# Alternating the two heads of a pair in three groups of small matmuls of a hybrid RWKV-7 block

## The chip, the cores and the metric

The kernel runs on one core of one Trainium2 chip. The metric is the device time of one execution in microseconds; the kernel before was timed three times, with a median of 1982.09 us (1978.47 to 1982.77). The profile is of one execution, and its times are counted from the first instruction of the span.

## The reference, cut to what matters

One layer of a diffusion backbone works on 256 context tokens and 256 latent tokens of 2048 features. A modulated norm is followed by one input projection, whose columns feed three groups: a bidirectional RWKV-7 recurrence (16 heads of 64 features), a short convolution and a Fourier mixing. Their outputs go through one output projection and a gated residual; a SwiGLU feed-forward layer with 5632 hidden features and a last norm follow. The change touches only the recurrence, which for each head and direction is

```
sa  = S · (-kk_t)
S   = S * w_t + sa ⊗ (kk_t * a_t) + v_t ⊗ k_t
y_t = S · r_t
```

with a 64 x 64 state S per head. The context's final states start the scans of the latent tokens; only the latent tokens need y.

## The kernel before, in words

The program has three stages: `phase_a` and `phase_kv` (modulation vectors, norms, first projections and keys), `recurrence`, and `phase_ffn`. Nearly all weights are multiplied as a high and a low part, three matmuls for each K-tile (`mm3`, `mm6`); `wblock` loads a block and splits it.

`recurrence` treats the heads in eight pairs, two heads of 64 features side by side on the 128 partitions (`HV[0]` and `HV[1]` are partitions 0 to 63 and 64 to 127). It goes over the eight pairs for the context stream (`s = 0`), then over the eight for the latent stream (`s = 1`): sixteen passes. The 256 tokens of a pass are cut into four chunks of 64 (`NC = 4`, `C = 64`). A pass has four running parts, written as Python generators: `rw_prep` (scaled keys and queries, Gram blocks, token-major values), two `rw_inverse` (the inverse of a triangular 64 x 64 matrix, one for each direction), and `rw_scan` (the state over the chunks), which for the latent stream ends in `rw_out` (the output y).

The loop of `recurrence` goes round by round: each running part makes one step, up to its next `yield`, and the number yielded is the share of TensorE, in microseconds, that the step is charged. `tick` then issues pieces of the filling products (value, query, gate, convolution, Fourier and output projections; tile `pj`) until the round has reached about 2.2 us (`ROUND_C`, `ROUND_L`). On TensorE the order of instructions is exactly the order in which the program issues them (`manual_schedule` for that engine); on the other engines a planner orders them by a simulated timeline. The charges are constants of the code: the token-major values have no charge of their own, the Gram blocks are charged 0.6 us (context) or 1.0 us (latent) a direction, `rw_out` 2.2 us.

Three places matter.

Lines 589 to 597 bring the values of a pair into token-major order, chunk by chunk, into the PSUM tile `pv` (tag `pp`): the even head by a matmul with a 64 x 64 unit matrix, the odd head by TensorE's transpose (line 595). ScalarE copies the tile out afterwards.

Lines 626 to 642 make the Gram blocks, direction by direction. For each head a PSUM tile `pg` (tag `pp`, two buffers for all users of the tag) takes four products, one a chunk, of 64 partitions by 128 stationary columns; then VectorE reads it, once for `ga` and for the latent stream once more for `mq`. So the first head's tile is read while TensorE works at the second head's. What takes a buffer of `pp` next (the other direction, then the transposed keys `pt` at line 645) waits for these reads.

`rw_out` (lines 831 to 850) sums, for each chunk, head and direction, two products into `py` (tag `acc`): `UV` times `MQ` with 128 rows and 64 columns of the array, and the state `w` times `AQ` with 64 rows and 64 columns. It goes through chunk, head, direction, and for each takes first the one, then the other.

Of the kernel before, what the change touches and what calls it, by code (L numbers as in the profile page):

```python
# [10 lines left out]
F32 = mybir.dt.float32  # L11
# [4 lines left out]
PSUM = bass.MemoryType.PSUM  # L16

P = 128
# [4 lines left out]
C = 64  # L23
# [35 lines left out]
class Cols:  # L59
    """Column map of a packed [128, n] array."""  # L60
# [140 lines left out]
class Builder:  # L201
# [12 lines left out]
    def wide(self, dt):  # L214
        """The place with room for two more columns a K-tile."""
        return self.t(self.cp, [P, KT, L + 2], dt, "XH0")
# [19 lines left out]
    def pull(self):  # L236
        """One piece of the filling products; its share of the tensor engine in us."""
        c = next(self.fill, None)
        return 0.0 if c is None else c
# [14 lines left out]
    def mm6(self, out, wh, wl, k, streams=(0, 1)):  # L254
        """One K-tile of w^T x for the streams side by side in one bank: only the bank's first
        matmul starts it, the other stream's first one finds its columns cleared."""
        ops = ((wh, self.XH), (wh, self.XL), (wl, self.XH))
        for i, (w, x) in enumerate(ops):
            for j, s in enumerate(streams):
                o = out[:, j * L:j * L + L]  # L260
                self.mm(o, w, x[s][:, k], k == 0 and i == 0 and j == 0,
                        k == KT - 1 and i == 2 and j == len(streams) - 1)
# [8 lines left out]
    def wblock(self, src, n, g, pool, tag="w32", bufs=None):  # L271
        """Loads n K-tiles of a 128-column weight block and splits them into hi and lo."""
        w = self.t(pool, [P, g, P], F32, tag, bufs)
        h = self.t(pool, [P, g, P], F32R, "whi")
        lo = self.t(pool, [P, g, P], F32R, "wlo")
        self.nc.sync.dma_start(w[:, :n], src)
        self.cnt += 1
        self.split(h[:, :n], lo[:, :n], w[:, :n], self.heng(self.cnt), self.leng(self.cnt))
        return h, lo

    def headsel(self, p, slot):
        """[16, 128] selector of the two heads of pair p."""
        t = self.adT[HN, P * slot:P * slot + P]
        self.nc.gpsimd.tensor_copy(t.rearrange("k (h i) -> k h i", h=2),
                                   self.cst("ident", 96 + 2 * p, 2, HN).unsqueeze(2).to_broadcast([16, 2, C]))
        return t

    def rsqrt(self, out, v, tmp):
        """out = 1/sqrt(v); one Newton step on top of sqrt and reciprocal."""
        nc = self.nc  # L290
        nc.scalar.activation(tmp, v, AF.Sqrt)
        nc.vector.reciprocal(out, tmp)
        nc.vector.tensor_tensor(tmp, out, v, op=ALU.mult)
        nc.vector.scalar_tensor_tensor(tmp, tmp, -0.5, out, op0=ALU.mult, op1=ALU.mult)
        nc.vector.scalar_tensor_tensor(out, tmp, 1.5, out, op0=ALU.add, op1=ALU.mult)

    def rms_add(self, ps, sq, k):
        """Adds K-tile k to the sums of squares, each quarter of the tokens in its own column tile."""
        m = sq.shape[1] // 4
        for q in range(4):  # L300
            self.mm(ps[32 * q:32 * q + 32, :m], self.ones32, sq[:, q * m:q * m + m], k == 0, k == KT - 1)

    def rms_finish(self, sums, pool, pspool, n, tag, scaled=False):
        """1/sqrt(mean square + eps) of n tokens, broadcast over the partitions in PSUM."""
# [15 lines left out]
    def conv3(self, out, ps, taps, groups, glen):  # L320
        """out[t] = w0 ps[t-1] + w1 ps[t] + w2 ps[t+1], zero outside each group."""
# [10 lines left out]
    def build(self, stop_after=None):  # L332
        tc, nc, a = self.tc, self.nc, self.a
        with ExitStack() as base:
# [6 lines left out]
            # hi and lo parts of the normalised tokens, context and latent  # L341
# [5 lines left out]
            with ExitStack() as kvs:  # L347
# [5 lines left out]
                # rows past the 96 of the LoRA: the norms of the keys and selectors of heads  # L353
                self.rn = self.wdT[HN]
                self.wend = self.t(kv, [P, NP, 2, C], F32, "wend")
                # keys of the context, two pairs a tile: their places later take the latent's "mq"
# [25 lines left out]
    def small_prep(self, pa):  # L382
        """Derived per-feature scalars and the masks of the block inverse."""
# [27 lines left out]
    def phase_a(self, st):  # L411
# [9 lines left out]
        # silu(c) as zero-padded stationaries  # L421
# [6 lines left out]
        # rms statistics of both streams  # L428
# [49 lines left out]
        # the banks of the last two blocks are needed first  # L478
# [55 lines left out]
    def value(self, p):  # L534
        # places: three of their own, then in turn those and the used-up keys of the context
# [19 lines left out]
    def rw_prep(self, st):  # L555
        """Scaled keys and queries, Gram blocks, values token-major."""
# [9 lines left out]
        # normalised keys, and [kk | k] mixed over the two heads  # L566
# [9 lines left out]
        # decay and in-context rate  # L576
# [9 lines left out]
        # values, token-major: [U; V] of the even head, [V; U] of the odd head  # L586
# [4 lines left out]
        for c in range(NC):  # L591
            cs = slice(c * C, c * C + C)
            for h in range(2):
                if h:
                    nc.tensor.transpose(pv[HV[0], cs], v32[HV[1], cs], cst("i64", rows=HV[1]))
                else:
                    self.mm(pv[HV[1], cs], v32[HV[0], cs], cst("i64", rows=HV[0]), True, True)
# [28 lines left out]
        for d in range(2):  # L626
            # Gram blocks
# [3 lines left out]
            st["MQ"].append(mq)  # L631
            for h in range(2):
                pg = T(self.pp, [P, NC, NQ * C], F32, "pp")
                for c in range(NC):
                    self.mm(pg[:, c], bk[HV[h], c].rearrange("p i t -> p (i t)"), aq[HV[h], c, :NQ * C], True, True)
# [7 lines left out]
        # token-major copies of the scaled keys  # L643
# [8 lines left out]
        # minus the intra-chunk part of the values  # L652
# [8 lines left out]
        if s:  # L661
            # bonus: (sum_j r (kf + kb) r_k) v
# [13 lines left out]
    def rw_decay(self, st, d, pl):  # L676
        """Tanh parts of direction d; returns what traces its running products of the decay."""
# [31 lines left out]
    def rw_inverse(self, st, d):  # L709
        """T = (I + M)^-1 of direction d: merges of blocks by two, then a Newton step in float32."""  # L710
# [55 lines left out]
    def rw_scan(self, st):  # L766
        """The state over the chunks, both directions side by side; st["W"]: the state before each step."""
# [8 lines left out]
        for i in range(NC):  # L776
            cc = (i, NC - 1 - i)
            # chunk cc[0] of the first direction and cc[1] of the second among the 2 * NC chunks
# [52 lines left out]
    def rw_out(self, st, Ws):  # L831
        """y of the latent stream, centred per head, and its squares."""
# [3 lines left out]
        for c in range(NC):  # L836
            for h in range(2):
                o = py[HV[h], c * C:c * C + C]
                for d in range(2):
                    w = Ws[c if d == 0 else NC - 1 - c]  # L840
                    self.mm(o, UV[:, h, d, c], MQ[d][:, h, c], d == 0, False)
                    self.mm(o, w[HV[h], d], AQ[d][HV[h], c, C:], False, d == 1)
# [5 lines left out]
        # the keys of this pair are used up: their place takes the squares  # L848
# [3 lines left out]
    def recurrence(self):  # L852
        """Both streams of all pairs, a step of each running part at a time, the filling products between."""
# [5 lines left out]
        # block-diagonal over the two heads; the zeros stay  # L859
# [43 lines left out]
    def fillers(self):  # L903
        """Gate, short-convolution and Fourier projections, a block at a time."""
# [52 lines left out]
    def group_norm(self, p0, p1):  # L957
        """Group norm, bonus and gate of the pairs p0..p1."""
# [30 lines left out]
    def out_proj(self):  # L989
        """x1 = x + ga1 (y @ w_out)."""  # L990
# [27 lines left out]
        # the last pair: one K-tile, four blocks of columns at a time; the statistics of x1 along with it  # L1018
# [4 lines left out]
        # the place of Y, used up, takes the hi part of x1 times the scale of its norm, and the shift beside it  # L1023
# [27 lines left out]
    def modvecs(self):  # L1051
        """ga1, sh2 and sc2, 512 columns at a time: products on the vector engine."""
# [18 lines left out]
    def mod_columns(self, i, pm, cols, ones, s):  # L1071
        """Sums over the partitions of 512 columns, plus the bias, as per-feature columns."""
# [9 lines left out]
    def modvec(self, i):  # L1082
        """512 columns of ga1, sh2, sc2 or ga2, as per-feature columns."""
# [11 lines left out]
    def modvec_end(self, i):  # L1095
        """The sums over the partitions."""
# [5 lines left out]
    def phase_ffn(self, st):  # L1102
# [11 lines left out]
        # the first two rows take the tokens before the norm's factor, which is known later; a product  # L1114
        # with the shift comes as one more token; the lo parts lie where the last rows' products go
# [10 lines left out]
        def gate_up(fs, xh, xl, norm=None):  # L1126
            """Gate and up products of the rows fs side by side, a group of K-tiles at a time."""
# [84 lines left out]
```

## Time and profile before

| | before |
|---|---|
| median of 3 runs | 1982.09 us |
| span of the profiled execution | 1980.6 us |
| TensorE matmuls busy | 1848.4 us (93%) |
| TensorE weight loads busy | 1679.4 us (85%) |
| VectorE busy | 1100.7 us (56%) |
| ScalarE busy | 831.1 us (42%) |
| GpSimd busy | 800.0 us (40%) |

Only the span of the profiled execution is recorded, not a time of its own around it; the median of the runs is 1.5 us above the span. A matmul's busy time is its latency: matmuls overlap in the array, so the distance between starts tells what one costs, and a merged line of the timeline holds several. An f32 product of the program is two instructions on TensorE (two weight loads and two matmuls), so that eight products of a Gram group show as sixteen. PE is TensorE's matmuls, PEld its weight loads, DVE is VectorE, ACT ScalarE, POOL GpSimd. PEclk is the clock that TensorE was granted: 1.00 is 2.4 GHz and 0.50 is 1.2 GHz.

### The profile page before, as it was taken

To read this page: it belongs to the slowest core of one execution; us is meant where nothing else is said; L and a number is where in the kernel's file an instruction comes from. 1 tells how busy PE (TensorE), PEld (TensorE's weight loads), DVE (VectorE), ACT (ScalarE), POOL (GpSimd) and SP (SyncE) were. 2 spreads that over 40 slices of the span, in tenths; PEclk is the share of its full clock that TensorE was granted. 3 is DMA by queue.
4 is the path that set the end of the run, shared out by engine and by line. 5 is a ranking of instruction groups with operands and counts; after the bars stand their busy time and mean duration, and the time that the engine had idled before them with its cause. 6 is when DMAs were issued, how large, how long until landed. Compare 5 with 4: busy or idle time off the path is not lost.

```text
span 1980.6 us, 44697 instructions
## 1 busy us (share of the span) xinstructions
PE 1848.4 (93%) x18488; PEld 1679.4 (85%) x18488; DVE 1100.7 (56%) x1883; ACT 831.1 (42%) x1657; POOL 800.0 (40%) x718
## 2 busy tenths in 40 slices
PE   7888999999999999899999888999999999999997
PEld 4777898888888887687887678999999899999997
DVE  4445257777678766656666378546454543332333
ACT  2213365555555554434443144343434344444442
POOL 1214455466577644535554144222222222223222
PEclk9999999999899988889898689999999999999998
DMA  8883223444444442343433025767676755556564
GB/s 326 292 269 122 78 84 120 139 140 150 133 157 150 132 125 90 104 141 109 115 113 110 24 85 157 247 194 250 194 234 192 225 181 182 184 188 191 185 194 133
DMA packets 139228, 318.75 MB, mean 161 GB/s; under 512 B 14224, under 2 KB 40464, under 8 KB 139024
## 3 DMA queue, kind: packets, MB, share of 16 engines
q1 hardware_dynamic: 137936, 314.84, 50.1%
q8 instruction: 145, 2.38, 0.5%
q10 hardware_dynamic: 1088, 1.05, 0.2%
q14 instruction: 59, 0.48, 0.1%
HBM read 313.74 MB, written 2.10 MB: 159 GB/s over the span
## 4 chain that ended last, share of the span: by engine, by line
PE 47%; DVE 8%; DMA 4%; ACT 1%; issue 1%; POOL 0%; DVEq 0%; SPq 0%; ACTq 0%; POOLq 0%
PE gu L233 20%; PE dn L233 12%; PE acc L233 5%; PE pj L233 5%; DMA XH<-wmb 3%; PE iv L233 2%; PE st L233 1%; PE pp L233 1%; DVE macc L1064 1%; DVE XH L1093 1%; DVE XL L1150 1%; DVE wlo L269 1%; DVE eb L730 0%; ACT whi L266 0%; DVE xn L1148 0%
## 5 line engine op out<-in xcount | busy, mean ns | idle before, releaser
L269 POOL TENSOR_TENSOR wlo<-w,whi 128x512 fp32r<-128x512 f32 (+2 forms) x309 | 518.8, 1682 | 783.4 <-ACT whi L266 746.8
L266 ACT CAST whi<-w 128x1024 fp32r<-128x1024 f32 (+2 forms) x472 | 400.7, 849 | 576.1 <-PE gu L233 192.9
L233 PE MATMUL gu<-XH,wlo 128*128 128x256 f32 (+1 forms) x1408 | 402.5, 286 | 13.0 <-DVE wlo L269 9.1
L233 PE MATMUL gu<-XH,whi 128*128 128x256 f32 (+1 forms) x1408 | 401.5, 285 | 4.1 <-ACT whi L266 4.0
L233 PE MATMUL gu<-XL,whi 128*128 128x256 f32 x1344 | 381.3, 284 | 0.0
L269 DVE TENSOR_TENSOR wlo<-w,whi 128x1024 fp32r<-128x1024 f32 (+1 forms) x175 | 208.3, 1191 | 301.9 <-ACT whi L266 295.3
L233 PE MATMUL pj<-XH,whi 128*128 128x256 f32 x1016 | 291.5, 315 | 2.9 <-DVE XL L998 1.3
L233 PEld LDWEIGHTS gu<-XH,wlo 128*128 128x128 f32 x1408 | 269.6, 192 | 15.7 <-DVE wlo L269 11.0
L233 PEld LDWEIGHTS gu<-XH,whi 128*128 128x128 f32 x1408 | 269.7, 192 | 5.1 <-ACT whi L266 4.8
L233 PE MATMUL pj<-XL,whi 128*128 128x256 f32 x1016 | 262.5, 287 | 0.6 <-DVE XL L269 0.6
L233 PE MATMUL pj<-XH,wlo 128*128 128x256 f32 x1016 | 262.3, 287 | 0.0
L233 PEld LDWEIGHTS gu<-XL,whi 128*128 128x128 f32 x1344 | 256.0, 190 | 0.2 <-DVE XL L1150 0.2
L233 PEld LDWEIGHTS pj<-XH,whi 128*128 128x128 f32 x1016 | 186.8, 196 | 14.2 <-issue 3.1
L233 PE MATMUL dn<-HL,whi 128*128 128x256 f32 x704 | 196.0, 278 | 0.0
L233 PE MATMUL dn<-HH,wlo 128*128 128x256 f32 x704 | 194.7, 277 | 0.0
L233 PE MATMUL dn<-HH,whi 128*128 128x256 f32 x704 | 194.4, 276 | 0.0
L233 PEld LDWEIGHTS pj<-XL,whi 128*128 128x128 f32 x1016 | 187.2, 196 | 2.5 <-issue 0.9
L233 PEld LDWEIGHTS pj<-XH,wlo 128*128 128x128 f32 x1016 | 186.2, 196 | 2.6 <-POOL whi L268 1.7
L1064 DVE SCALAR_TENSOR_TENSOR macc<-wm,sc,macc 128x512 f32<-128x512 f32 x180 | 170.8, 949 | 4.5 <-DMA wm<-wmb 3.7
L233 PEld LDWEIGHTS dn<-HL,whi 128*128 128x128 f32 x704 | 132.2, 188 | 1.4
L233 PEld LDWEIGHTS dn<-HH,wlo 128*128 128x128 f32 x704 | 132.2, 188 | 0.3 <-POOL wlo L269 0.2
L233 PEld LDWEIGHTS dn<-HH,whi 128*128 128x128 f32 x704 | 132.1, 188 | 0.0
(312 smaller groups left out, 3027.4 us busy)
## 6 DMA issues: line engine op xcount, KB each, us to landing
w<-wgu SPq DMA_DIRECT2D x176, 512.0 KB, 4.5
wm<-wmb SPq DMA_DIRECT2D x192, 256.0 KB, 3.0
w<-wdn SPq DMA_DIRECT2D x80, 512.0 KB, 4.5
w<-wib SPq DMA_DIRECT2D x148, 256.0 KB, 3.2
wm<-wma SPq DMA_DIRECT2D x64, 512.0 KB, 7.7
XH<-wmb SPq DMA_DIRECT2D x64, 256.0 KB, 4.1
w<-wout SPq DMA_DIRECT2D x48, 256.0 KB, 3.2
wa<-wia SPq DMA_DIRECT2D x16, 416.0 KB, 8.8
```

Source lines behind the costliest of these rows:

```text
L233: self.last = self.nc.tensor.matmul(out, lhsT=lhsT, rhs=rhs, start=start, stop=stop)
L266: he.copy(hi, src)
L269: le.tensor_tensor(lo, src, hi.bitcast(F32), op=ALU.subtract)
L1064: V.scalar_tensor_tensor(acc, w, self.sc[:, k, 1:2], acc, op0=ALU.mult, op1=ALU.add)
L1093: nc.vector.scalar_tensor_tensor(acc, w, self.sc[:, k, 1:2], acc, op0=ALU.mult, op1=ALU.add)
L1150: V.scalar_tensor_tensor(XL[:, k], xn, bias, XH[:, k].bitcast(F32), op0=ALU.add, op1=ALU.subtract)
```

## The change

Comments are removed throughout, which changes no instruction. What is left:

```diff
-                if h:
-                    nc.tensor.transpose(pv[HV[0], cs], v32[HV[1], cs], cst("i64", rows=HV[1]))
-                else:
-                    self.mm(pv[HV[1], cs], v32[HV[0], cs], cst("i64", rows=HV[0]), True, True)
+                self.mm(pv[HV[1 - h], cs], v32[HV[h], cs], cst("i64", rows=HV[h]), True, True)
...
+            pgs = [T(self.pp, [P, NC, NQ * C], F32, "pp") for _ in range(2)]
+            for c in range(NC):
+                for h in range(2):
+                    self.mm(pgs[h][:, c], bk[HV[h], c].rearrange("p i t -> p (i t)"), aq[HV[h], c, :NQ * C], True, True)
             for h in range(2):
-                pg = T(self.pp, [P, NC, NQ * C], F32, "pp")
-                for c in range(NC):
-                    self.mm(pg[:, c], bk[HV[h], c].rearrange("p i t -> p (i t)"), aq[HV[h], c, :NQ * C], True, True)
+                pg = pgs[h]
...
         for c in range(NC):
-            for h in range(2):
-                o = py[HV[h], c * C:c * C + C]
-                for d in range(2):
-                    w = Ws[c if d == 0 else NC - 1 - c]
-                    self.mm(o, UV[:, h, d, c], MQ[d][:, h, c], d == 0, False)
-                    self.mm(o, w[HV[h], d], AQ[d][HV[h], c, C:], False, d == 1)
+            for d in range(2):
+                w = Ws[c if d == 0 else NC - 1 - c]
+                for h in range(2):
+                    self.mm(py[HV[h], c * C:c * C + C], UV[:, h, d, c], MQ[d][:, h, c], d == 0, False)
+                for h in range(2):
+                    self.mm(py[HV[h], c * C:c * C + C], w[HV[h], d], AQ[d][HV[h], c, C:], False, d == 1)
```

The odd head's values now go through a matmul with the unit matrix, like the even head's, so that all products of the group are of one kind and the heads alternate. The Gram blocks of both heads go chunk by chunk into two tiles that are held at the same time, and VectorE's reads stand behind all of them. In `rw_out` the products of one kind stand together for the two heads, so the kind changes half as often. The number of f32 products is the same but for the four transposes of each pass, which become four products. No yield, charge, buffer count or DMA is changed.

## Rows read from the trace of the kernel before

**Rows 1.** Windows: length, busy PE, PEld, DVE, ACT, POOL (instructions); clock, DMA share, GB/s.
```profile
242.00:700.00 458.00, 438.71 (x5473) 391.42 (x5473) 333.04 (x648) 254.32 (x644) 278.66 (x310) 0.95 0.42 133
700.00:1065.00 365.00, 340.08 (x3768) 282.42 (x3769) 238.89 (x495) 157.55 (x401) 181.64 (x214) 0.89 0.38 114
1065.00:1180.00 115.00, 100.47 (x899) 77.76 (x895) 57.86 (x122) 38.24 (x90) 34.54 (x31) 0.77 0.20 59
1180.00:1980.60 800.60, 767.09 (x6498) 759.33 (x6498) 365.70 (x437) 319.28 (x395) 234.34 (x99) 0.98 0.62 195
```
**Rows 2.** The eight stretches of `rw_out`, tile `acc` alone (windows; last line their sum).
```profile
1081.60:1094.70 13.10, 12.98 (x64) 9.16 (x64) 0.00 (x0) 0.01 (x1) 0.50 0.00 0
...
sum 84.50, PE 83.88 PEld 60.17 DVE 0.00 ACT 0.05; mean PE 10.48 PEld 7.52 DVE 0.00 ACT 0.01
```
**Rows 3.** `rw_out` of the first latent pass on PE (timeline: start, length, instructions).
```profile
720.78 0.33 PE L233 MATMUL acc<-mq,UV 128*64 128x64 f32 x2
721.04 0.33 PE L233 MATMUL acc<-aq,wend 64*64 64x64 f32 x2
...
725.40 0.47 PE L233 MATMUL acc<-mq,UV 128*64 128x64 f32 x2
725.81 0.47 PE L233 MATMUL acc<-aq,w 64*64 64x64 f32 x2
```
**Rows 4.** Its second half and what follows it, with the clock (windows).
```profile
725.00:730.00 5.00, 5.00 (x27) 3.58 (x28) 0.15 (x1) 0.00 (x0) 0.00 (x0) 0.54 0.55 181
730.00:735.00 5.00, 5.00 (x55) 4.05 (x57) 1.98 (x5) 2.77 (x8) 1.15 (x3) 0.50 0.00 0
```
**Rows 5.** Token-major values of the first pass on PE (timeline).
```profile
249.74 0.32 PE L233 MATMUL pp<-consts,vc 64*64 64x64 f32 x2
250.00 0.24 PE L595 MATMUL pp<-consts,vc 64*64 64x64 f32 x1
250.17 0.33 PE L233 MATMUL pp<-consts,vc 64*64 64x64 f32 x2
...
251.46 0.50 PE L233 MATMUL pj<-XH,whi 128*128 128x256 f32 x2
```
**Rows 6.** Groups on PE whose two heads alternate already, and what follows each (timeline).
```profile
267.74 1.15 PE L233 MATMUL pp<-UV,ga 64*64 64x64 f32 x32
268.81 0.39 PE L233 MATMUL pj<-XH,whi 128*128 128x256 f32 x1
...
306.53 0.45 PE L233 MATMUL st<-Z,e 64*64 64x64 f32 x8
306.91 0.29 PE L233 MATMUL iv<-i,im 128*128 128x64 f16 x4
...
309.46 0.45 PE L233 MATMUL st<-UV,bkt 128*64 128x64 f32 x8
309.85 0.29 PE L233 MATMUL iv<-de,im 128*128 128x64 f16 x4
```
**Rows 7.** Gram groups on PE: full clock, half clock after a wait, latent pass (timeline).
```profile
258.04 1.60 PE L233 MATMUL pp<-aq,bk 64*128 64x64 f32 x16
259.57 0.51 PE L233 MATMUL pj<-XH,whi 128*128 128x256 f32 x2
...
390.83 1.09 PE L233 MATMUL iv<-e,idm 64*64 64x64 f32 x16 [3.10 <-DVE idm L757]
391.85 2.88 PE L233 MATMUL pp<-aq,bk 64*128 64x64 f32 x16
394.66 0.58 PE L233 MATMUL pj<-XH,whi 128*128 128x256 f32 x1
...
804.25 1.79 PE L233 MATMUL pp<-aq,bk 64*128 64x128 f32 x16 [0.39 <-DVE mq L640]
```
**Rows 8.** VectorE's last read of the Gram group before that one (timeline).
```profile
804.36 0.42 DVE L640 TENSOR_TENSOR mq<-pp,consts 128x256 f32<-128x256 f32 x1
```
**Rows 9.** The end of the half clock behind rows 7's 3.10 us wait (windows).
```profile
400.00:405.00 5.00, 5.00 (x34) 4.66 (x34) 2.04 (x6) 0.93 (x3) 2.77 (x4) 0.54 0.11 37
```

## The prediction

> **What bounds the kernel now.** I read the stretches of the span first, then the timeline of TensorE at the three edited places, then VectorE beside it and the granted clock. [rows 1] shows that the feed-forward stage after 1180 us is TensorE's (767.1 of 800.6 us busy) and holds nothing of the change. In the context part of the recurrence (242 to 700 us) TensorE is busy 438.7 of 458 us while VectorE has 333 and ScalarE 254; in the latent part up to 1065 us it is 340.1 of 365, and in the last stretch 100.5 of 115. So for most of the recurrence TensorE's instruction stream is what ends last, and because its order is fixed by hand, a group that becomes shorter pulls everything behind it forward, until an engine that it waits for is late. The waits there are now are small: 19 us in the context part, 40 us in the latent. The clock matters too: 0.95, 0.89 and 0.77 in these three stretches, against 0.98 afterwards.
>
> What the edits attack is visible when groups are compared. In the output block each product is two matmuls, and 0.26 us pass from one product's start to the next [rows 3]. In a group where the heads alternate, 32 matmuls of the same 64 x 64 shape take 1.07 us up to the next product, 0.033 us each [rows 6]: a quarter. The eight of `st<-Z` take 0.38 us with a change of shape behind them; with 0.033 us for each the shape change is worth about 0.12 us.
>
> **The change, part by part.**
>
> *Output block.* The eight blocks are 83.9 us busy; the tail of each overlaps what follows, so about 82 us of stream [rows 2]. Now there are 32 runs of two matmuls, each run of another shape than the one before. Afterwards there are 16 runs of four. The price of a run of four is in no row; two matmuls cost 0.257 us [rows 3] and eight cost 0.385 [rows 6], and the line through these gives 0.30. From below: eight less four of 0.033 is 0.25. From above, if the two heads don't overlap: one matmul alone costs 0.17 (250.00 to 250.17 in [rows 5]), so the second of its product adds 0.09, and four cost 0.43. I take 0.30, the nearest rows being of the very shapes used here: 128*64 and 64*64 in [rows 6] cost the same. A block is then 16 x 0.30 = 4.8 us at the full clock, where it would be 8.2 now. It is more than 8.2 now since the clock goes to half inside the block, 4.6 us after its start (0.257 becomes 0.40 at 725.40 in [rows 3], with the granted clock at 0.54 in [rows 4]); the block that is at half clock throughout takes 13.0 [rows 2]. With one block at half clock (7.5) and seven at 4.8, the sum is 41 us: 41 us saved, between 25 (0.43 a run, 7 x 6.9 + 9) and 47.
>
> The Trainium skill speaks against the products with 128 rows: "TensorE: Matmul & The Clock Gate", section "Part 3: Packing small matmuls", says that a weight load runs beside a matmul in flight only when the two use different groups of rows, and the two heads of `UV` differ in columns alone. By that rule those runs would be at 0.43 and a block at 5.8 us, 8 us less saved in all. The trace disagrees: `st<-UV,bkt`, which differs in columns alone, takes 0.39 us for eight, `st<-Z` 0.38 [rows 6].
>
> After the block the clock stays at half in the next 5 us [rows 4]. What stands there would lose about 2.2 us less of a block each if the fall were gone; with a block that ends about where the clock falls now, I count a third of 8 x 2.2, 6 us, between 0 and 18.
>
> *Values.* A group takes 1.72 us, 249.74 to 251.46 [rows 5], because matmul and transpose alternate: 0.26 and 0.17 us. Afterwards it is 16 matmuls of one shape, heads alternating: 16 x 0.033 + 0.12 = 0.65 us, though a product has two matmuls where a transpose has one. That saves 1.1 us, and over 16 passes 17.6 us; from the other side (no overlap at all) it would be 16 x 0.09 + 0.12 = 1.56 us, 2.6 saved. I take the former, since `pp<-UV,ga` has this very shape and pattern.
>
> *Gram blocks.* A context group takes 1.53 us, 258.04 to 259.57, and 2.81 at the half clock [rows 7]: 0.096 us a matmul. No row has two heads that share all 128 columns and differ in rows alone, so the cost lies between 0.033 as in [rows 6] (0.65 us a group) and no overlap (1.53). If each head keeps its pace and the two go side by side, a matmul costs 0.048 and the group 0.85; I take that. The nearest row, `pp<-UV,ga`, has half the columns, and twice 0.033 would be 0.066, 1.15 a group. Of 16 context groups, each saves 0.7: 11 us, and I add 2 us for those at half clock, of which 391.85 is one (2.81 to about 1.6). Bounds for context: 0 to 16.
>
> The Trainium skill, in the same page's section "LDWEIGHTS (loading the stationary operand)", gives a load's time as its columns divided by 1.2 in ns, 107 ns for 128. If loads came one after another, 16 of them would fill 1.7 us and alternating would save nothing here. But then 32 loads of 64 columns would fill 1.7 us as well, and [rows 6] has 1.07 us for them with their matmuls, so loads of two heads do run beside each other at least where rows and columns both differ; where rows alone differ, no run shows it.
>
> In the latent passes the group takes about as long (1.72 us, 804.25 to its next neighbour at 805.97, with the wait at its second head), and VectorE reads each tile twice, 0.42 us a read; the last read of the group before ends at 804.78 [rows 8]. Both tiles must be free for the next direction's second product now, where the first tile was enough for half a group before. In [rows 7] the group at 804.25 already had to wait 0.39 us for `mq`. As the reads now start when both heads are done, which is about when the first head was done before, the reads end as before, and this group could start no sooner than 804.8. There most of the gain is lost; in passes with more filling work between the two directions it isn't. I count 4 us for the 16 latent groups, between -8 (no overlap; reads 0.8 us later, half of it on the path of 16 groups, 6 us, and some clock) and 11.
>
> *New waits.* The rounds in which the three groups lie are longer than their charge, so even shortened they are no shorter than their neighbours, and those hardly wait in the context part. In the latent part the inverse's steps (VectorE's `idm`, `w`, `rhs`) are late already. I take back a fifth of the latent savings (41 + 9 + 4 + 6 = 60): 12 us. On the other engines the planner may order differently; I count that at nothing, within a few us either way.
>
> **Sum.** 41 + 6 + 17.6 + 13 + 4 - 12 = 70 us. The profiled span is 1980.6 us and the median of the runs 1.5 above it, so 1982.1 - 70 = 1912 us.
>
> **The rivals.**
>
> *Waits take over.* Where the stream gets shorter, the chain through VectorE (sx, idm, mq) becomes the pace of the latent passes, and half of its 60 us comes back: 17.6/2 + 13 + 30 = 52, 1930 us. For it: 40 us of waits there already [rows 1] and the wait in [rows 7]. Against: during an output block VectorE has next to nothing to do (0.15 us in 5, [rows 4]), so at the greatest saving it is ready. The last two blocks have no filling work and are the surest.
>
> *The clock stays up.* If the output blocks no longer pull the clock down, and the Gram groups follow at full clock, 12 us more of recovery and fewer waits: 70 + 12 + 8 = 90, 1892 us. For it: in [rows 3] the clock falls only when the block has run 4.6 us. Against: it is also at half after a plain wait (3.10 us in [rows 7], still 0.54 in [rows 9]).
>
> *Less overlap than in the rows.* Weight loads of heads that share rows or columns go one after another: Gram groups stay at 1.53 us (0 in the context part, -4 in the latent with the later reads), and the `UV` runs at 0.43 save 33 instead of 41: 17.6 - 4 + 33 + 3 - 8 = 42, 1940 us. For it: no row has heads that differ in rows alone. Against: the eight of `st<-UV,bkt` in [rows 6]. The Trainium skill's two rules above point this way.
>
> *Slower.* TensorE, ahead of VectorE, stands idle in more passes, and each wait like the 3.10 us of [rows 7] costs a stretch at half clock: 14 us from 391 to 405, half of it lost, about 7 us [rows 7, 9]. To eat 70 us it needs at least ten new stretches, one in most passes; with twelve, 1982 - 70 + 84 = 1996 us. For it: the context part has had such a fall behind that wait. Against: in most passes the round after the shortened group is full of filling work.
>
> **How the numbers follow.** Forecast 1912 us: 0.45. Waits take over, 1930: 0.22. Clock stays up, 1892: 0.15. Less overlap, 1940: 0.13. Slower, 1996: 0.05. The range from 1882 to 1948 us takes in the four faster cases with a few us of their bounds, and leaves out the slower one and the tails. A difference under 0.2%, 4 us, can't be told from none. Faster: 0.93; same: 0.02; slower: 0.05.
>
> **What would show it.** Values groups of 0.65 us and no transposes at line 595; output blocks of 4.8 us with 16 runs, and the clock at their end; Gram groups near 0.85 us (1.5 would mean that heads with the same columns don't overlap); waits of `pp` for `mq` above their present few us. It would be wrong if the output blocks keep 8 us or more, or if TensorE's idle time in the recurrence grows by more than 30 us.

## The result and the profile after

The changed kernel takes 1894.6 us (median of four runs, 1889.0 to 1905.2) against 1980.3 us for the kernel before, run beside it: a ratio of 0.957, with a 95% interval of 0.954 to 0.960. It is 86 us faster where 70 were forecast, and inside the range; of the times on record before, the one it comes nearest to is not the forecast of 1912 us but the 1892 us of the rival in which the clock stays up. Measured again in a later series the ratio was 0.957 (0.955 to 0.960).

The page of the changed kernel, its span and busy times:

```profile
span 1890.0 us, 44826 instructions
PE 1740.1 (92%) x18552; PEld 1592.8 (84%) x18552; DVE 1107.6 (59%) x1883; ACT 830.3 (44%) x1657; POOL 802.3 (42%) x718
```

Only TensorE has less to do: 108 us of matmul time and 87 us of weight loads are gone. VectorE, ScalarE and GpSimd are as busy as before to within 7 us. The 64 more matmuls are the transposes that became products.

The recurrence, in the changed kernel up to 1090 us, where it is as far as the kernel before is at 1180 us; this answers to the first three lines of [rows 1] taken together. First the kernel before, then the changed one (windows: length, then PE, PEld, DVE, ACT, POOL busy, clock, DMA share, GB/s):

```profile
242.00:1180.00 938.00, 879.26 (x10131) 751.60 (x10129) 629.79 (x1263) 450.11 (x1135) 494.84 (x554) 0.91 0.38 117
```
```profile
242.00:1090.00 848.00, 771.52 (x10183) 666.18 (x10182) 636.00 (x1263) 449.22 (x1134) 496.02 (x554) 0.96 0.42 129
```

This is the account that the rest of the document uses. TensorE is busy 108 us less, and stands idle 76.5 us (848.0 - 771.5) where it stood 58.7 (938.0 - 879.3): 18 us more. The difference is the 90 us by which this execution is shorter. The granted clock of the stretch went from 0.91 to 0.96. After the recurrence nothing changed (765.7 us busy of 800 from 1090 us on, as in the last line of [rows 1]).

The output block, which answers to [rows 2]: first block, the slowest, and the sum of the eight (windows, tile `acc` alone):

```profile
701.00:705.30 4.30, 4.23 (x64) 3.14 (x64) 0.00 (x0) 0.00 (x0) 1.00 0.75 216
...
1008.10:1012.70 4.60, 4.45 (x64) 3.31 (x64) 0.00 (x0) 0.00 (x0) 1.00 0.01 4
...
sum 35.30, PE 34.38 PEld 25.27 DVE 0.00 ACT 0.01; mean PE 4.30 PEld 3.16 DVE 0.00 ACT 0.00
```

From 83.9 us to 34.4 us, and the clock is 1.00 in all eight, where one block was at half clock throughout and in the other seven the clock fell on the way (mean clock 0.66 to 0.80) [rows 2 to 4]. The runs of four, the values and a Gram group on TensorE's timeline, which answer to [rows 3], [rows 5] and the first lines of [rows 7]:

```profile
701.07 0.34 PE L233 MATMUL acc<-mq,UV 128*64 128x64 f32 x4
701.34 0.33 PE L233 MATMUL acc<-aq,wend 64*64 64x64 f32 x4
701.60 0.34 PE L233 MATMUL acc<-mq,UV 128*64 128x64 f32 x4
...
248.57 0.68 PE L233 MATMUL pp<-consts,vc 64*64 64x64 f32 x16
249.18 0.39 PE L233 MATMUL pj<-XH,whi 128*128 128x256 f32 x1
...
255.76 1.11 PE L233 MATMUL pp<-aq,bk 64*128 64x64 f32 x16
256.80 0.51 PE L233 MATMUL pj<-XH,whi 128*128 128x256 f32 x2
```

Starts are what to read: a run of four takes 0.26 us (0.30 forecast), a group of values 0.61 (0.65), a Gram group 1.04 (0.85). So runs were forecast too dear and Gram groups too cheap.

The `UV` runs, whose heads differ in columns alone, cost the same 0.26 us as the state's runs, whose rows differ too. The Trainium skill, "TensorE: Matmul & The Clock Gate", section "Part 3: Packing small matmuls", says that weight loads overlap with matmuls in flight only when their row groups differ. This trace does not agree: the 0.26 us of the `UV` runs is against 0.37 us for a run of one head (below).

The sixteen loads of a Gram group are done within its 1.04 us. The Trainium skill, in the same page's section "LDWEIGHTS (loading the stationary operand)", gives the time of one load, about 107 ns for 128 columns by its formula. That the loads follow one another, which would fill 1.7 us, was a supposition of the prediction and not the page's; it is this that doesn't hold.

### The profile page after: what moved, and what is told of

Same layout as the page of the kernel before. It is cut to its first block, busy times and chain, and to the rows that moved or that the text cites. A ratio compares the mean times of both kernels' runs of the same rounds, so it can differ in the third digit from the quotient of the medians.

```text
span 1890.0 us, 44826 instructions
## 1 busy us (share of the span) xinstructions
PE 1740.1 (92%) x18552; PEld 1592.8 (84%) x18552; DVE 1107.6 (59%) x1883; ACT 830.3 (44%) x1657; POOL 802.3 (42%) x718
## 4 chain that ended last, share of the span: by engine, by line
PE 42%; DVE 9%; DMA 6%; issue 2%; ACT 2%; POOL 0%; SPq 0%; DVEq 0%; ACTq 0%
PE gu L233 18%; PE dn L233 13%; DMA XH<-wmb 6%; PE pj L233 4%; PE acc L233 2%; PE iv L233 2%; PE st L233 2%; PE pp L233 1%; DVE XH L1092 1%; DVE macc L1063 1%; DVE XL L1149 1%; DVE HL L1120 0%; ACT whi L266 0%; DVE eb L729 0%; DVE xn L1147 0%
## 5 line engine op out<-in xcount | busy, mean ns | idle before, releaser
L233 PE MATMUL pj<-XH,whi 128*128 128x256 f32 x1016 | 286.4, 310 | 5.6 <-DVE XL L997 2.5
L233 PEld LDWEIGHTS gu<-XH,wlo 128*128 128x128 f32 x1408 | 268.4, 191 | 13.2 <-DVE wlo L269 10.4
L233 PE MATMUL pj<-XL,whi 128*128 128x256 f32 x1016 | 258.3, 282 | 0.6 <-DVE XL L269 0.6
L233 PE MATMUL pj<-XH,wlo 128*128 128x256 f32 x1016 | 258.0, 282 | 0.0
L233 PEld LDWEIGHTS pj<-XH,whi 128*128 128x128 f32 x1016 | 182.4, 191 | 16.9 <-ACT whi L266 3.1
L233 PEld LDWEIGHTS pj<-XL,whi 128*128 128x128 f32 x1016 | 182.6, 192 | 2.4 <-issue 0.9
L233 PEld LDWEIGHTS pj<-XH,wlo 128*128 128x128 f32 x1016 | 181.7, 191 | 2.6 <-POOL whi L268 1.7
```

Source lines behind the costliest of these rows:

```text
L233: self.last = self.nc.tensor.matmul(out, lhsT=lhsT, rhs=rhs, start=start, stop=stop)
```

## The experiments

The theory at this point: each group's saving on TensorE's stream lands in the time, the clock adds to the output block, and waits take some back. The rivals: that waits or a shared clock effect make the parts overlap, and that the clock or the number of shape changes, rather than the alternation, is what was bought.

**Each part alone.** Three kernels, each the kernel before with one hunk of the change.

> The kernel before with the values edit alone (the odd head by a matmul with the unit matrix). Theory (each group's saving in TensorE's stream lands in the time): sixteen groups from 1.72 to 0.61 us, 18 us, about 1962 us against 1980. Rival (waits take the place of what is saved): half or less of it, 1971 us or more, and TensorE's waits for VectorE and ScalarE in the recurrence grow by the other half.

Measured: 1955.0 us, ratio 0.987 (0.983 to 0.992): 25 us. More than the theory's 18, and the rival is out: TensorE's idle time in the recurrence rose by 6 us only (65.0 of 913 us, where it was 58.7). Its recurrence (windows):

```profile
242.00:1155.00 913.00, 847.98 (x10183) 729.93 (x10182) 630.99 (x1267) 449.49 (x1134) 493.89 (x553) 0.92 0.39 120
```

> The kernel before with the Gram edit alone (both heads chunk by chunk into two tiles). Theory: 0.5 us for each of 16 context groups at the full clock and about 4 us in the latent passes, where VectorE's reads set the pace: 12 us, 1968 us. Rival (both tiles held, reads later): the latent groups lose as much as the context groups gain, 1978 to 1982 us, with more waits for mq. Second rival (clock): the half-clock stretches that lie at the context's Gram groups go as well, 20 us more, 1950 us.

Measured: 1968.7 us, ratio 0.996 (0.993 to 0.999): 8 us against the kernel before beside it. Nearer to the theory than to the first rival; the second (a large clock effect) is out.

> The kernel before with the output edit alone. Theory: eight blocks from 10.3 to 4.2 us, 48 us, and some 10 us from the clock behind them, 1922 us; blocks at the full clock. Rival (the clock stays up only with the other two edits): the blocks lose part of it to the half clock, 5.5 us each and the stretches behind them stay, 1942 us.

Measured: 1923.1 us, ratio 0.971 (0.966 to 0.976): 57 us, where the theory has 48 + 10. Idle time did not grow (56.8 us of 874):

```profile
242.00:1116.00 874.00, 817.20 (x10102) 706.72 (x10100) 628.04 (x1260) 448.15 (x1131) 494.10 (x551) 0.94 0.40 124
```

The parts add up: 25 + 8 + 57 = 90 against 86.

**Values and Gram together, without the output edit.**

> The values and Gram edits without the output edit. Theory (the three parts add up): 25 and 8 us as alone, 1946 us against 1979, 51 us over the changed kernel's 1895. Rival (the parts share one saving, the same half-clock stretches): 1935 us or less, or 1958 us or more.

Measured: 1948.5 us, ratio 0.986 (0.983 to 0.990): 30 us, additive within the interval. The output edit is worth another 54.

**Is it the alternation, or the changes of shape?** In the output block, the same 16 runs of four, but each run of one head:

```diff
             for h in range(2):
                 o = py[HV[h], c * C:c * C + C]
                 for d in range(2):
-                    w = Ws[c if d == 0 else NC - 1 - c]
                     self.mm(o, UV[:, h, d, c], MQ[d][:, h, c], d == 0, False)
+                for d in range(2):
+                    w = Ws[c if d == 0 else NC - 1 - c]
                     self.mm(o, w[HV[h], d], AQ[d][HV[h], c, C:], False, d == 1)
```

> The kernel before with the output block's products of one kind together (both directions' UV products, then both directions' state products) but head by head, without alternation: 16 runs of four as in the edit. Theory (alternation lets two heads run side by side): a run of four costs 0.43 us without it, a block 6.9 us at the full clock and about 7.5 with its fall, 1957 us. Rival (only the changes of shape cost): a run costs 0.26 to 0.30 us as in the edit, and the time is that of the output edit alone, 1922 us.

Measured: 1929.4 us, ratio 0.973 (0.967 to 0.979), 53 us of the 57. TensorE's timeline of this kernel:

```profile
724.32 0.45 PE L233 MATMUL acc<-mq,UV 128*64 128x64 f32 x4
724.69 0.44 PE L233 MATMUL acc<-aq,w 64*64 64x64 f32 x4
725.06 0.45 PE L233 MATMUL acc<-mq,UV 128*64 128x64 f32 x4
```

A run of four without alternation takes 0.37 us, less than the 0.43 I had as the price of no overlap, and the alternation brings it to 0.26. A block is 5.9 us, and no matmul in any of them lasts longer than 0.27 us, as at the full clock. On the stream the alternation should be worth 16 x 0.11 x 8 = 14 us. The recurrence of this kernel has them:

```profile
242.00:1131.00 889.00, 832.41 (x10091) 722.17 (x10090) 625.18 (x1256) 445.95 (x1128) 487.59 (x551) 0.94 0.39 122
```

TensorE is busy 15 us more than with the output edit alone (832.4 against 817.2) and idle as long (56.6 and 56.8). But these are single executions, the medians differ by 6 and the intervals overlap, so that share isn't resolved in time. What is shown is that putting products of one kind together gives most of it. The theory's 1957 us was wrong.

The same question for the values: the odd head by matmul, but head after head.

```diff
-        for c in range(NC):
-            cs = slice(c * C, c * C + C)
-            for h in range(2):
...
+        for h in range(2):
+            for c in range(NC):
+                cs = slice(c * C, c * C + C)
+                self.mm(pv[HV[1 - h], cs], v32[HV[h], cs], cst("i64", rows=HV[h]), True, True)
```

> The kernel before, with the odd head's values by matmul as in the edit but head after head, four chunks each, without alternation or transposes. Theory (both the change of kind and the alternation count): 16 matmuls at 0.064 us as in the output block without alternation, and 0.12: 1.14 us a group instead of 0.61, 0.6 us saved of 1.72, 9 us and a few of the clock, 1968 us. Rival (the transposes alone cost): as the values edit, 1955 us.

Measured: 1960.1 us, ratio 0.991 (0.988 to 0.994), 18 us. The first group, on TensorE:

```profile
246.62 0.96 PE L233 MATMUL pp<-consts,vc 64*64 64x64 f32 x16
247.51 0.50 PE L233 MATMUL pj<-XH,whi 128*128 128x256 f32 x2
```

0.89 us: of the 1.11 us that the edit saves in a group, 0.83 come from making all products of one kind and 0.28 from the alternation. The rival is nearer: most of the 25 us, 18 of them, came without alternation, with the switching between matmul and transpose gone. The 7 us between the two kernels are within their intervals, so here too the alternation isn't resolved in time.

**Fewer shape changes still.** The changed kernel with all `UV` products of the pass first, then all state products, so that two runs of 32 remain:

```diff
         for c in range(NC):
             for d in range(2):
-                w = Ws[c if d == 0 else NC - 1 - c]
                 for h in range(2):
-                    self.mm(py[HV[h], c * C:c * C + C], UV[:, h, d, c], MQ[d][:, h, c], d == 0, False)
+                    self.mm(py[HV[h], c * C:c * C + C], UV[:, h, d, c], MQ[d][:, h, c], c == 0 and d == 0, False)
+        for c in range(NC):
+            for d in range(2):
+                w = Ws[c if d == 0 else NC - 1 - c]
                 for h in range(2):
...
```

> The changed kernel, with the output block in two runs: all UV products of the pass, heads alternating, then all state products (only the first product of each head starts its part of the bank). Theory (what costs in the block is the change of shape, 0.12 us each, and the matmuls 0.033): the block goes from 4.2 to about 2.3 us, eight blocks 15 us, 1879 us. Rival (waits take the place: after the block the steps of the inverse and the next round's VectorE work are late): half of it or less, 1887 us or more.

The changed kernel ran once more on the same chip, for comparison:

> The three edits together, the changed kernel once more, beside the next two on one chip. Both theories: the ratio of the first measurement, 0.957 (1894 us against 1980).

Measured: 1890.8 us, ratio 0.956 (0.953 to 0.958), against 1895.2 us, 0.957 (0.955 to 0.960): 4 us, within the intervals. TensorE's timeline of the first, from the block to the first wait behind it:

```profile
700.33 1.15 PE L233 MATMUL acc<-mq,UV 128*64 128x64 f32 x32
701.41 0.33 PE L233 MATMUL acc<-aq,wend 64*64 64x64 f32 x4
...
702.40 0.63 PE L233 MATMUL iv<-d,ga 64*64 64x64 f32 x16
...
705.77 0.45 PE L233 MATMUL iv<-e,idm 64*64 64x64 f32 x8 [1.52 <-DVE idm L756]
```

VectorE over the same stretch (timeline):

```profile
699.32 5.39 DVE L1065 SCALAR_TENSOR_TENSOR macc<-wm,sc,macc 128x512 f32<-128x512 f32 x5
...
705.30 0.41 DVE L756 TENSOR_TENSOR idm<-consts,iv 128x256 f32<-128x256 f32 x1
```

Its recurrence, and its seventh block (windows):

```profile
242.00:1086.00 844.00, 756.81 (x10189) 658.26 (x10187) 635.88 (x1263) 448.76 (x1134) 497.82 (x554) 0.96 0.42 129
...
1008.20:1012.30 4.10, 4.10 (x68) 3.88 (x68) 0.42 (x1) 0.91 (x3) 0.00 (x0) 0.50 0.02 4
```

The block is 2.07 us where 2.3 were expected, and at most 2.2 in seven of the eight passes; the seventh lies at half clock throughout and takes 4.05, hardly less than the 4.28 of the changed kernel. The stream is 14.7 us shorter than the changed kernel's (756.8 against 771.5). But idle time is 87.2 us where it was 76.5: 10.7 of the 14.7 us came back as waits, the first of them 1.52 us for the inverse's `idm` right behind the block. VectorE makes `idm` late because a row of `macc` steps from before the block holds it until 704.7. Behind six of the eight blocks TensorE waits 0.5 to 1.9 us. The rival holds. This is where the output block stops being the bound. The median is the lowest of the study, but the kernel is not shown to be faster than the changed one.

**The clock.** First try: the old block, with filling work pulled in between its chunks.

```diff
+            if c < NC - 1:
+                for _ in range(4):
+                    self.credit -= self.pull()
```

> The kernel before with its output block's order unchanged (32 runs of two), but four pieces of the filling products pulled in after each of the first three chunks, and charged against the rounds that follow; the sum of work is the same. Theory (part of what the output edit gave is the clock, which the old block pulls down): the old block's products stay at 0.26 us instead of 0.40, 2 us a block, and the stretches of half clock behind the blocks go, some 2 us more: 30 us, 1950 us. Rival (the clock is not what the block costs): the block's products are as before, and the time is 1978 us or more, since the filling work is missing in the rounds after it.

Measured: 1984.8 us, ratio 1.003 (1.001 to 1.005), 6 us slower. It doesn't settle the matter. In the first block the products between waits ran at 0.26 us, but two of the pulled pieces waited 0.9 and 1.2 us for their own inputs (TensorE's timeline):

```profile
726.91 1.13 PE L233 MATMUL pj<-XL 128*128 128x256 f32 x4 [0.91 <-ACT XL L942]
729.24 3.48 PE L233 MATMUL pj<-XL 128*128 128x256 f32 x8 [1.20 <-DVE XL L948]
```

The clock was 0.91 to 1.00 in seven of the eight blocks; in the seventh, into which no piece was pulled, it was 0.50. So the products ran as the theory has it, and the time did not follow. Over the latent part (700 to 1180 us) the clock is 0.88 against 0.86 and TensorE is busy as long as before (440.2 against 440.6 us): what the blocks gained was lost elsewhere, and where was not traced. The filling work can't be moved without moving what it covers.

Second try: the changed kernel, its block padded to the old length with full-array products into a part of the bank that is overwritten later (two after each chunk).

```diff
+            for _ in range(2):
+                self.mm(py[:, L:], self.cst("bmean"), self.klat[:, p], True, True)
```

> The changed kernel, with two more products after each chunk of the output block (128 x 128 by 256 columns, into the part of the bank that is overwritten later): the block is about as long as the old one at the full clock (4.2 + 8 x 0.5 = 8.2 us), but the array is full in it. Theory (the clock is part of what the output edit gave): the blocks stay at full clock, 32 us over the changed kernel, 1927 us, some 20 us under the kernel with the values and Gram edits alone. Rival (the block's length is all that counts, or the time goes to waits that the length hides): as the kernel without the output edit, 1946 us; if waits took over the savings, under 1915 us.

Measured: 1924.9 us, ratio 0.973 (0.970 to 0.977); the theory has 1927. The first block of the padded kernel and what follows, then its seventh block (windows):

```profile
699.60:708.30 8.70, 8.70 (x88) 6.03 (x88) 5.40 (x8) 1.47 (x5) 2.60 (x4) 1.00 0.69 212
708.30:713.30 5.00, 5.00 (x102) 4.10 (x101) 3.88 (x11) 2.56 (x8) 3.45 (x5) 1.00 0.08 25
...
1027.60:1042.30 14.70, 14.70 (x84) 9.41 (x81) 0.42 (x1) 1.01 (x3) 0.00 (x0) 0.50 0.00 1
```

The second half of the first block of the kernel without the output edit, and what follows:

```profile
703.20:708.20 5.00, 5.00 (x31) 3.62 (x32) 0.61 (x2) 0.00 (x0) 0.00 (x0) 0.51 0.49 164
708.20:713.20 5.00, 5.00 (x67) 4.21 (x63) 2.32 (x6) 2.85 (x8) 1.57 (x3) 0.50 0.01 3
```

The padded block has about the length of the old one at full clock (8.46 us from 699.66 to 708.12, against 32 x 0.257 = 8.2). In seven of the eight padded blocks the clock is 1.00, in the first also in the 5 us behind it; the seventh begins at half clock, stays there and takes 14.6 us, so that the theory's "the blocks stay at full clock" holds for seven. In the other kernel the clock is 0.51 in the first block's second half and 0.50 behind it. The recurrence of the padded kernel, then of the one without the output edit:

```profile
242.00:1122.00 880.00, 807.35 (x10298) 689.10 (x10297) 631.76 (x1262) 448.56 (x1133) 490.22 (x552) 0.96 0.40 123
```
```profile
242.00:1144.00 902.00, 827.80 (x10177) 708.24 (x10175) 633.51 (x1263) 449.61 (x1134) 493.41 (x553) 0.93 0.39 121
```

The times are 24 us apart (1924.9 and 1948.5, intervals apart), and waits don't explain it: TensorE is idle 72.7 us in the one and 74.2 in the other. The clock differs in every run, not only in the profiled one: over the whole span it is 0.968 to 0.975 padded, 0.950 to 0.957 without the output edit. So of the output edit's 54 us over the values and Gram edits, about 24 are the clock. The other 30 are what padding costs over the changed kernel (1924.9 - 1895.2): the block's length at full clock, and in it some 6 us that the seventh block lost at half clock. The clock's share lies between 24 and 30 us. What in the padded block keeps the clock up, fewer turns between kinds or the full-array products, was not separated.

**Gram blocks, context and latent.** The changed kernel, with the old order in the one or the other kind of pass (`if s`, or `if not s`, around the old loop):

> The changed kernel, but the Gram groups of the latent passes as before (one head after the other, tile by tile); the context's alternate. Theory (the latent groups are set by VectorE's reads and gain about 4 us): 1898 us. Rival (holding both tiles costs as much as alternating gives there): no difference from the changed kernel, or 2 to 5 us less, 1890 us. Second rival (the latent groups gain their full 0.5 us each): 1902 us.

Measured, old order in the latent passes: 1904.8 us, ratio 0.962 (0.960 to 0.965) beside 0.957 (0.955 to 0.960) of the changed kernel on the same chip: 10 us. The second rival, the full gain, comes nearest. This kernel differs from the changed one in the latent Gram groups alone, whose products are of one kind in both orders: here the alternation itself is resolved in time.

> The changed kernel, but the Gram groups of the context passes as before, one head after the other; the latent ones alternate. Theory (0.5 us for each of 16 context groups on TensorE's stream): 8 us over the changed kernel, 1903 us. Rival (they are hidden by the waits behind them): no difference, 1895 us. Second rival (they bring half-clock stretches with them): 1908 us or more.

Measured, old order in the context passes: 1892.2 us, ratio 0.957 (0.954 to 0.960): no difference. The rival is right. Windows of the context part of the changed kernel, of this one, and of the changed kernel run again, which reaches the same point 3 us later:

```profile
242.00:606.00 364.00, 342.51 (x4616) 306.78 (x4614) 276.39 (x529) 216.54 (x549) 224.54 (x254) 0.99 0.45 139
```
```profile
242.00:606.00 364.00, 345.94 (x4606) 311.67 (x4606) 268.99 (x529) 215.39 (x548) 227.96 (x253) 0.99 0.44 138
```
```profile
242.00:609.00 367.00, 344.37 (x4617) 308.81 (x4616) 276.98 (x528) 216.61 (x549) 225.90 (x254) 0.98 0.45 138
```

With the old order TensorE is busy 3.4 us more and idle 3.4 us less in the same 364 us. The two profiles of the changed kernel are themselves 1.9 us apart in busy time and 1.1 in idle time (21.5 and 22.6, against 18.1 with the old order), so that the sizes are rough, but the waits are fewer with the old order against both. What the context's Gram groups save is waited for. For the latent passes the same two views, of the changed kernel run again and of the one with the old order there:

```profile
609.00:1089.00 480.00, 427.80 (x5567) 358.79 (x5563) 353.03 (x729) 229.93 (x582) 266.45 (x298) 0.94 0.41 121
```
```profile
609.00:1096.00 487.00, 436.19 (x5559) 368.45 (x5557) 353.56 (x733) 230.70 (x583) 264.02 (x299) 0.94 0.40 119
```

Here the alternation takes away 8.4 us of busy time and adds only 1.4 us of waits.

## Why the prediction was right, and where not

*TensorE's stream as the bound* held: 108 us less on TensorE gave 90 us less time in the profile. It had its limits close by: the next 14.7 us, in the output block, gave 4, and what the context's Gram groups save gave nothing.

*Output block.* Forecast 41 us of block, measured 49.5 (83.9 to 34.4). A run cost 0.26 where 0.30 was taken from a line between two and eight matmuls; the lower end, eight less four of 0.033, was the right guide. And no block was left at half clock, where I had kept one. The clock was rightly a term of its own: 82 - 8 x 8.2 = 16 us inside the blocks and 6 behind them were in the sum, less 2.7 for the one block that I left at half clock: some 20 together, and the padded kernel puts it at 24 to 30. The price of "no overlap", 0.43, was too high: one matmul alone was read from a transpose [rows 5], and a run of one head measured 0.37.

*Values.* Forecast 17.6, measured 25 alone (17 to 34 by the interval). The group's price was right (0.61 for 0.65). The profile of that kernel has 31.3 us less busy time in the recurrence (848.0 us), where 16 x 1.1 are 18; no group of the kernel before lay at half clock, since its transposes took 0.24 us in every record. The other 13 us lie outside the edited groups. What is seen to change there is the clock: 0.92 against 0.91 in the recurrence, and over the whole span 0.954 to 0.957 in all four runs against 0.944 to 0.950 of the kernel before beside it. That it is the cause is likely but was not isolated.

*Gram blocks.* The sum of this step was 17, measured 8 to 10, and its two halves were the wrong way round. The context groups got 13 us in my sum and gave nothing that can be measured; the latent ones got 4 and gave 10. Three readings were wrong. First, the size: a matmul at 0.048 and a group of 0.85, measured 1.04. Twice the 0.033 of a group with half the columns, which stood beside it, gives 0.066 and 1.15. The 0.048 is half of 0.096, and 0.096 is no head's own pace. Read matmul by matmul (the two interleaved rows of eight starts taken for the two heads), a head's matmuls start 0.11 us apart in both kernels, and the second head's first one starts 0.50 us after the first head's before (258.54 and 258.04), 0.01 us after it now. So the two heads ran beside each other in part already, now they do in full, and that 0.50 us is the whole gain of a group. Second, "those hardly wait in the context part": they do as soon as the groups are shorter. The 16 context groups, from each start to the next product's, went from 29.6 to 16.8 us, about the 13 forecast (four lay at half clock before, none in this profile), but in time the waits behind them took it back. Third, I judged the latent groups by one pass, where VectorE's reads stood in the way. They do: in the changed kernel's pass at 763 us the second group waits twice.

```profile
762.98 1.16 PE L233 MATMUL pp<-aq,bk 64*128 64x128 f32 x16
765.07 0.46 PE L233 MATMUL pp<-aq,bk 64*128 64x128 f32 x2 [0.93 <-DVE mq L639]
765.73 1.13 PE L233 MATMUL pp<-aq,bk 64*128 64x128 f32 x14 [0.21 <-DVE mq L639]
```

But over all passes the old order is only 1.4 us less idle, and the waits of `pp` for `mq`, which I named as a sign, went from 5.0 to 6.5 us only.

*New waits.* Forecast 12 us, 18 in the profile, and spread otherwise: 8 us of them in the context part, where I had none (21.5 idle of 364 us after, 13.2 of 383 to the same point before). The argument that VectorE has next to nothing to do during an output block was read from the block's second half [rows 4]; in the 5 us before, the first half, it was busy 4.86:

```profile
720.00:725.00 5.00, 5.00 (x42) 3.80 (x40) 4.86 (x5) 1.69 (x4) 3.03 (x3) 1.00 0.79 220
```

In the changed kernel's first block it is busy 3.8 of 4.1 us, and behind a block of 2.07 us TensorE waits for it, as the kernel with two runs shows.

*The rivals.* Waits that take over: not in this change, but they are next, as the kernel with two runs of 32 shows. The clock staying up: it does in the output blocks, and at 1894.6 us the time is 3 us from this case and 17 from my forecast; but its second part, fewer waits, did not come, there were 18 us more. Less overlap than in the rows: no; heads that share rows overlap, and heads that share all columns too. Slower through new half-clock stretches: no; the waits grew and the clock of the recurrence still rose from 0.91 to 0.96.

The account of the misses, in TensorE's busy time in the recurrence: the sum had 82 us before waits, and 108 were saved. The output edit alone took away 62 (879.3 to 817.2; the blocks' 49.5 and 12.6 outside them, where the sum had 6), the values alone 31 where it had 17.6, the Gram groups 12 (8.4 and 3.4) where it had 17: 105 together. So most of what the sum lacked, some 20 of 26 us, lies outside the edited groups (12.6 - 6 and 31 - 18). What is seen to change there is the granted clock. An estimate of its worth: if every stretch is at one of the two levels, a mean of 0.91 over 938 us is some 169 us at half clock, and 0.96 over 848 us some 68; work at half clock took 1.6 to 1.8 times as long (0.257 to 0.40, 1.53 to 2.81), so that 100 us less of it are some 40 us saved, where the sum had about 22 (20 with the output block, 2 with the Gram groups). So the clock beyond the blocks is the term that was put too low, as far as is known; which edit brings how much of it was isolated for the output block alone. Against these stand 6 us more waits than forecast. That the time fell inside the range is owed in part to luck: the context's Gram groups, 13 us of the sum, gave nothing, and what was gained outside the groups made up for them.

## What to carry to other kernels

Small products of different array shapes, or matmuls and transposes, that take turns on TensorE pay at each turn: sort by kind first, then alternate halves of the array within a kind. In the output block and the values the sorting gave most (53 of 57 us and 18 of 25), the alternation less than the runs resolve; where the kind was one already, in the latent Gram groups, the alternation gave 10 us. Price such a block by starts on the timeline, at both clock levels, and look at the clock in the 5 us behind it: a block that brings the clock down costs there as well. And when a group on the bounding engine has been cut, do the account of busy and idle time for the stretch before cutting it again: here the second cut gave back three quarters as waits.

## What the runs showed of the hardware

A change of array shape costs about 0.15 us at the full clock, as an estimate from two runs: a run of four takes 0.262 us and a run of 32 on average 1.04 (700.33 to 702.40 for two), so 0.028 us for a matmul and 0.15 for the turn. The Trainium skill, "TensorEngine Tiling (Array Packing)", section "Key Properties", says that a change of tiling mode drains the engine; it gives no price. Whether a drain is what takes the 0.15 us, the trace doesn't show.

Matmuls of 64 rows that share all 128 columns run fully beside each other when their rows differ: a head's matmuls start 0.11 us apart, whether the other head's run beside them or not, and two heads of eight take 1.04 us with their starts together against 1.53 with the second 0.50 us later. The old order, one head after the other, already overlapped them in part; that is why the gain is a third and not a half.

A TensorE that is busy all the time can still fall to 1.2 GHz: in the old block there is no wait, yet the clock was 0.54 over 725 to 730 us, in its second half, and 0.50 in the 5 us that follow [rows 4]. The padded block, as long and with full-array products among them, stayed at 1.00 in seven of eight passes; in the one that began at half clock the same products did not bring it back within its 14.6 us.
